# Conditioning in steps of 512 columns, and the first MLP's shift beside the first output projection

## The chip, the cores and the metric

The kernel runs on one core of a Trainium2 chip. Its time is the device time of one execution in microseconds (us). Matrix products run on TensorE (PE; its weight loads are shown apart as PEld), elementwise work on VectorE (DVE), ScalarE (ACT) and GpSimd (POOL). SyncE (SP) issues all DMA transfers here, in one queue and in order. Work moves between DRAM, the on-chip SBUF (128 partitions) and PSUM, which takes the results of matmuls in eight banks.

## What is computed

One inference step of a two-layer encoder on 1024 prompt tokens and 32 sample tokens, with 1024 features. Layer 0 has an mLSTM mixer, layer 1 banded attention, and each has a squared-ReLU MLP with 4096 hidden features. Every sublayer is modulated by six vectors (two shifts, two scales, two gates) that come from a conditioning vector c, of which there is one for the prompt and one for the sample:

```python
def ada_mod(c, w, b):
    return jax.nn.silu(c) @ w + b

for l in range(DEPTH):
    sh1, sc1, g1, sh2, sc2, g2 = jnp.split(ada_mod(c, p['w_ada'][l], p['b_ada'][l])[:, None, :], 6, axis=-1)
    u = x * (1 + sc1) + sh1
    y = mixer(u) if l == 0 else attention(u, k_sh, v_sh)   # ends with the output projection
    x = layer_norm(ALPHA * x + (1 + g1) * y, p['ln_g'][l, 0], p['ln_b'][l, 0])
    u = x * (1 + sc2) + sh2
    f = jnp.square(jax.nn.relu(u @ p['w_up'][l])) @ p['w_down'][l]
    x = layer_norm(ALPHA * x + (1 + g2) * f, p['ln_g'][l, 1], p['ln_b'][l, 1])
```

w_ada[l] has 1024 rows and 6144 columns, six parts of 1024. A further matrix of 2048 columns, w_ada_kv, conditions the keys and values that layer 1 reads. The parts are numbered 0 to 5 in the order sh1, sc1, g1, sh2, sc2, g2: the first MLP's shift is part 3 of layer 0.

## The kernel before

Activations are kept transposed, features on the partitions and tokens along the columns, in three token blocks of 384, 384 and 288 (TBS). Large products are made in three float32r passes (`proj`, L118 to L120): each operand is split into a high part, made by ACT (L89), and a remainder, made by DVE or POOL (L90).

**Conditioning.** Parts 0 and 1 of layer 0 are needed first, and TensorE makes them (`ada_start`). All other parts are made by `ada_cols` (L223) on DVE. It works on two chunks of 128 columns at a time: a block of 512 rows x 256 columns of the matrix is loaded (L229, 512 KB, into `raw`), and for each of its four row chunks and each of the two conditions the 256 columns are multiplied by one value of silu(c) per partition and added to an accumulator (L239 the first time, L236 after that). After the second block a transpose by 32 x 32 squares (L243) and a sum (L244) leave 16 columns in `cx`; when four such groups are in `cx`, four small matmuls with the matrix `sel` (L250) finish the sum over the partitions, and L253 adds the bias and writes eight chunks of `ada`. `ada_fix` makes 1 + scale and (1 + gate) / alpha; `combine` (L268) merges the layer norm's gain and bias with scale and shift into `comb`.

**Side work.** What is not the main sequence of products is written as generators under `Flow`. A generator yields the time, in us, that TensorE should spend on other work before its next step; the main sequence calls `flow.tick(us)` after each piece (1 us by default), and each tick moves a generator by at most one step. `flow.finish(g)` puts out all that is left of one. This sets the order in which the program is written down; the framework's scheduler then orders each engine's instructions and inserts the waits.

**The order around the change.** In the mixer (to about 440 us in the profile) query/key, value and output-gate projections alternate with `mlstm`, the chunks of the previous head. The rest of layer 0's conditioning, parts 2 to 5, runs beside it as `ada_l0` (L730): one buffer of the ring `wc`, named ada_room, is cut into accumulator, transposed copy and one block of loaded weights, and ADA_C gives the yields, 2.0 after each load and 2.0 at the end of a group. L790 finishes all that is left of it. Next, `combine` runs (L1044), and the first output projection `out_proj` (L958) begins: it loads its eight weight blocks (raw_oa) through the ring `raw`, which has three buffers, loads the residual `acc` (L808) and walks the three token blocks, with eight tiles of 24 matmuls for each. After a tile, L947 adds it to the residual, and `flow.tick(n / 96)` counts 4 us, or 3 in the last block. After a block its `norm` (L825) is started as side work: a sum over the features on DVE, the mean by a matmul (L843), squares, the variance by a matmul, and then in four steps the normalised residual and its modulation by `comb` (L324 to L329), which writes U, the input of the MLP; W00 holds its yields. `tmp_t` gives out five temporary buffers. The MLP's first products `up` read U in the order of the blocks.

The conditioning of layer 1 and of the keys and values (`ada_rest`, L1058) is side work of the first MLP, with loads through `raw`, temporaries from `tmp_t` and the yields ADA_B.

The lines of the program that the change touches:

Of the kernel before, what the change touches and what calls it, by code (L numbers as in the profile page):

```python
# [8 lines left out]
F32 = mybir.dt.float32  # L9
F32R = mybir.dt.float32r  # L10
AF = mybir.ActivationFunctionType
ALU = mybir.AluOpType
# [5 lines left out]
KC = D // P                     # feature chunks  # L18
TP = 1024                       # prompt tokens
TS = 32                         # sample tokens  # L20
T = TP + TS
NT = T // P + 1                 # token tiles, the last one holds the sample
# [4 lines left out]
NH = 4                          # mLSTM heads  # L27
CH = 128                        # mLSTM chunk
NCK = TP // CH
SAMPLE_C = NCK                  # index of the sample's mLSTM chunk  # L30
# [3 lines left out]
def segs(t0, n):  # L34
    """Pieces (offset, length, conditioning column) of a token block."""
# [11 lines left out]
class Flow:  # L47
    """Side work, as generators that yield how long (us) the tensor engine should do something else first."""
# [27 lines left out]
def trunk_kernel(ctx: ExitStack, tc: tile.TileContext, a, o):  # L76
# [6 lines left out]
    # ------------------------------------------------------------------ tools  # L83
# [3 lines left out]
    def split(dst_h, dst_l, src, eng=None):  # L87
        """dst_h + dst_l == src exactly, both parts in float32r."""
        nc.scalar.copy(dst_h, src)  # L89
        (eng or nc.vector).tensor_sub(dst_l, src, dst_h.bitcast(F32))  # L90

    def wtile(name, srcs, ncols=256, pool=None, eng=None, between=None):
        """A block of 4 contraction chunks x ncols columns, split. srcs: (dst slice fn, dram ap)."""
# [12 lines left out]
    def wblock(name, src, r0, c0, eng=None):  # L106
        """rows r0..r0+511, columns c0..c0+255 of src."""
# [3 lines left out]
    def proj(ps, n, halves, j, mov):  # L111
        """ps[:, :n] = the 128 columns j of the weight halves times mov(hl, k), three f32r passes."""
# [9 lines left out]
    # one activation table set serves every function used below  # L122
    nc.scalar.preload_act_table_set("natural_log_exp_and_others")

    # -------------------------------------------------------------- constants
    ident = cp.tile([P, P], F32, name="ident")
    make_identity(nc, ident)
    sel = cp.tile([P, 32], F32, name="sel")             # sel[32 a + j, j] = 1
# [8 lines left out]
    # x0T / x1T: the residual stream, transposed, while the mixers need its room  # L137
# [6 lines left out]
    # ------------------------------------------------- per-feature parameters  # L144
# [10 lines left out]
    comb = cp.tile([P, 3, KC, 2, 2], F32, name="comb")   # fused norm scale / shift per (norm, chunk, cond)  # L155
# [29 lines left out]
    def bank(name):  # L185
        """All eight banks in turn, for the phases that need no classes of them."""
# [19 lines left out]
    # silu(c) = c * exp(min(c, 0) - ln(1 + exp(-|c|)))  # L206
# [1209 lines left out]
```

## Time and profile before

| | us |
|---|---|
| median of 3 runs | 2562.2 |
| lowest, highest | 2561.2, 2562.53 |
| profiled execution, first to last instruction (its span) | 2562.6 |
| PE busy | 2493.5 |
| DVE busy | 1686.0 |
| ACT busy | 895.3 |
| POOL busy | 339.5 |

For the profiled execution the span is the only time of its own that is recorded; it lies 0.4 us above the median of the timed runs. Times are counted from the first instruction of the span. In a row of a group of instructions stand line, engine, operation, the tiles it writes and reads, shape and count, then the time busy and the mean duration in ns, and then the idle time of the engine just before them with what ended it. In a row of waits stand who waited, for whom, the sum in us, how often, and the longest. In a row of windows stand the stretch, then busy time and number of instructions of PE, PEld, DVE, ACT and POOL, the granted clock of TensorE as a share of full speed, the busy share of the DMA engines, and GB/s; asked for one tile, it has the engines alone that work on it. In a row of the timeline stand start, duration, engine, line, operation, and in brackets the idle time before it and what ended it.

### The profile page before, as it was taken

How to read it: one execution, taken by the hardware profiler on the slowest of the kernel's cores; microseconds unless marked ns; L12 is line 12 of the kernel's file. 1: busy time of each engine (PE TensorE's matmuls, PEld its weight loads, DVE VectorE, ACT ScalarE, POOL GpSimd, SP SyncE). 2: the span in 40 equal slices, each digit the busy share in tenths (PEclk: the TensorE clock that was granted, in tenths of full speed). 3: DMA queues.
4: the chain of work that ended last, by engine and by line, in shares of the span. 5: the costliest groups of instructions: out<-in, count | busy, mean ns of one | idle time of the engine just before them, and what ended most of it. 6: DMA issues, size and time to landing. Idle time of an engine off the chain costs nothing.

```text
span 2562.6 us, 40022 instructions
## 1 busy us (share of the span) xinstructions
PE 2493.5 (97%) x15784; PEld 2371.5 (93%) x15784; DVE 1686.0 (66%) x3825; ACT 895.3 (35%) x1903; POOL 339.5 (13%) x455
## 2 busy tenths in 40 slices
PE   7999999999999999999989999999999999999998
PEld 3899899999999999999989876789999999999997
DVE  3899999778679678766696676637644334343437
ACT  3654456242212211221256566625411211221212
POOL 0111100251000000000053143405300000000003
PEclk9999999999999999999999999999999999999999
DMA  7532323412224224223113400051111111111101
GB/s 235 161 91 88 93 82 110 142 34 84 89 91 131 92 86 137 83 91 120 58 68 116 97 4 1 1 159 34 50 50 42 42 50 42 49 51 41 44 31 68
DMA packets 192064, 201.20 MB, mean 79 GB/s; under 512 B 9337, under 2 KB 180749, under 8 KB 191877
## 3 DMA queue, kind: packets, MB, share of 16 engines
q1 hardware_dynamic: 191876, 198.65, 25.4%
q8 instruction: 124, 2.03, 0.3%
q14 instruction: 64, 0.52, 0.1%
HBM read 183.38 MB, written 17.60 MB: 78 GB/s over the span
## 4 chain that ended last, share of the span: by engine, by line
PE 82%; DVE 7%; DMA 2%; ACT 2%; issue 1%; POOL 1%; SPq 0%; ACTq 0%; DVEq 0%; POOLq 0%
PE dn L118 10%; PE up L118 9%; PE dn L120 9%; PE up L119 9%; PE up L120 9%; PE dn L119 9%; PE pv L1275 3%; PE s L1225 2%; PE pt L1255 2%; DVE ada_room L236 1%; DMA ada_room<-in_w_ada_dram 1%; PE o L118 1%; PE o L120 1%; PE o L119 1%; PE q L118 1%
## 5 line engine op out<-in xcount | busy, mean ns | idle before, releaser
L118 PE MATMUL dn<-h,w_dn 128*128 128x384 f32 (+2 forms) x1568 | 505.9, 323 | 0.0
L120 PE MATMUL dn<-h,w_dn 128*128 128x384 f32 (+2 forms) x1568 | 501.9, 320 | 0.0
L119 PE MATMUL dn<-h,w_dn 128*128 128x384 f32 (+2 forms) x1568 | 497.8, 318 | 0.0
L955 DVE SCALAR_TENSOR_TENSOR acc<-dn,ada,acc 128x384 f32<-128x384 f32 (+5 forms) x536 | 243.7, 475 | 235.8 <-PE dn L120 234.1
L118 PEld LDWEIGHTS dn<-h,w_dn 128*128 128x128 f32 x1568 | 294.5, 188 | 0.8 <-PE yt L914 0.2
L119 PEld LDWEIGHTS dn<-h,w_dn 128*128 128x128 f32 x1568 | 294.2, 188 | 0.1
L120 PEld LDWEIGHTS dn<-h,w_dn 128*128 128x128 f32 x1568 | 294.0, 188 | 0.0
L995 DVE TENSOR_TENSOR r<-r 128x384 f32<-128x384 f32 (+1 forms) x192 | 104.2, 544 | 282.7 <-ACT h L994 282.1
L993 ACT ACTIVATE r<-up 128x384 f32<-128x384 f32 (+1 forms) x192 | 88.9, 463 | 470.6 <-PE up L120 456.2
L118 PE MATMUL up<-U,w_up 128*128 128x384 f32 (+1 forms) x768 | 250.2, 326 | 0.0
L119 PE MATMUL up<-U,w_up 128*128 128x384 f32 (+1 forms) x768 | 249.1, 324 | 0.0
L120 PE MATMUL up<-U,w_up 128*128 128x384 f32 (+1 forms) x768 | 248.7, 324 | 0.0
L118 PE MATMUL up<-u,w_up 128*128 128x384 f32 (+1 forms) x768 | 248.5, 324 | 0.0
L119 PE MATMUL up<-u,w_up 128*128 128x384 f32 (+1 forms) x768 | 248.4, 323 | 0.0
L120 PE MATMUL up<-u,w_up 128*128 128x384 f32 (+1 forms) x768 | 248.3, 323 | 0.0
L89 ACT CAST w_up<-raw_up 128x1024 fp32r<-128x1024 f32 x64 | 66.9, 1049 | 411.1 <-PE dn L120 274.3
L236 DVE SCALAR_TENSOR_TENSOR aacc<-rada,cs,aacc 128x256 f32<-128x256 f32 x448 | 190.4, 478 | 0.0
L118 PEld LDWEIGHTS up<-U,w_up 128*128 128x128 f32 x768 | 145.1, 189 | 0.1
L120 PEld LDWEIGHTS up<-U,w_up 128*128 128x128 f32 x768 | 145.1, 189 | 0.0
L119 PEld LDWEIGHTS up<-U,w_up 128*128 128x128 f32 x768 | 145.1, 189 | 0.0
L120 PEld LDWEIGHTS up<-u,w_up 128*128 128x128 f32 x768 | 144.3, 188 | 0.0
L119 PEld LDWEIGHTS up<-u,w_up 128*128 128x128 f32 x768 | 144.2, 188 | 0.0
(317 smaller groups left out, 5403.0 us busy)
## 6 DMA issues: line engine op xcount, KB each, us to landing
raw_up<-in_w_up_dram SPq DMA_DIRECT2D x64, 512.0 KB
raw_dn<-in_w_down_dram SPq DMA_DIRECT2D x64, 512.0 KB
rada<-in_w_ada_dram SPq DMA_DIRECT2D x48, 512.0 KB
ada_room<-in_w_ada_dram SPq DMA_DIRECT2D x32, 512.0 KB
rada<-in_w_ada_dram SPq DMA_DIRECT2D x32, 256.0 KB
rada<-in_w_ada_kv_dram SPq DMA_DIRECT2D x16, 512.0 KB
acc<-xsp SPq DMA_DIRECT2D x4, 1536.0 KB
rc<-rc_d SPq DMA_DIRECT2D x8, 528.0 KB
```

Of the source, the lines that this page charges most:

```text
L89: nc.scalar.copy(dst_h, src)
L118: nc.tensor.matmul(ps, wh, mov(0, k), start=(k == 0), stop=False)
L119: nc.tensor.matmul(ps, wh, mov(1, k), start=False, stop=False)
L120: nc.tensor.matmul(ps, wl, mov(0, k), start=False, stop=(k == nk - 1))
L236: nc.vector.scalar_tensor_tensor(acc[:, cnd], raw[:, k], sc, acc[:, cnd], op0=ALU.mult, op1=ALU.add)
L955: nc.vector.scalar_tensor_tensor(xs, ps[:, off + o:off + o + mm_], gate[:, fc, cnd:cnd + 1], xs, op0=ALU.mult, op1=ALU.add)
L993: nc.scalar.activation(r, ps[:, :n], AF.Relu)
L995: nc.vector.tensor_mul(r, r, r)
L1225: nc.tensor.matmul(s[:, b, :w], qst, kk[i][:, g, k0 + j0:k0 + j0 + w], start=(i == 0), stop=(i == 1))
L1255: nc.tensor.transpose(pt[:kp, j - j0, pr * P:(pr + 1) * P], ps_[pr][:, j * P:j * P + kp], ident)
L1275: nc.tensor.matmul(pv[64 * e:64 * e + 64, :nq], V[:kp, vt0 + j, g * 64:(g + 1) * 64], pts[e][:kp, j, :nq], start=(j == 0), stop=(j == nt - 1))
```

## The change

`ada_cols` works on four chunks of 128 columns at a time. A load is 256 rows x 512 columns, still 512 KB, and there are four of them to a group in place of two. For each of the two row chunks of a load, and each condition, one operation on 512 columns takes the place of operations on 256. Each condition has an accumulator of its own, and its own transpose and sum at the end of a group, so that two groups now fill `cx` and lead to the `sel` matmuls. Of the yields two are left: step[0] after each load, step[1] at the end of a group; the one in the middle of a block is gone.

Beside the mixer `ada_l0` makes parts 2, 5 and 4 only, in this order. Its transposed copies now lie where the loaded weights lie in the room. Part 3, the first MLP's shift, is made by a new generator, `ada_shift`, which is side work of the first output projection, loads through the ring `raw` and takes its temporaries from `tmp_t`. It ends with the `combine` that stood ahead of the projection. The norms of that projection get a hook, `before`, that finishes `ada_shift` just ahead of their modulation. `ada_rest` uses the new `ada_cols` with yields of 5.0 and 2.0. Everything else in the diff is comments.

```diff
-    def ada_cols(src, c0, base, nch, mk, tmp_f, step, raw_f=raw_tile):
-        """ada[:, base..base+nch-1] = silu(c) @ src[:, c0..c0+128*nch-1] + bias, multiplied on the vector engine."""
-        for j in range(0, nch, 2):
-            acc = tmp_f([P, 2, 256], f"aacc_{base}_{j}")
-            for half in range(2):
-                raw = raw_f([P, 4, 256], f"rada_{base}_{j}_{half}")
-                nc.sync.dma_start(raw, src[512 * half:512 * half + 512, c0 + j * P:c0 + (j + 2) * P].rearrange(
+    def ada_cols(src, c0, base, nch, mk, tmp_f, step, raw_f):
+
+
+        cx3 = cx.rearrange("p g b -> p (g b)").rearrange("p (g b) -> p g b", g=2)
+        for j in range(0, nch, 4):
+            accs_ = [tmp_f([P, 512], f"aacc{cnd}_{base}_{j}", cnd) for cnd in range(2)]
+            for quarter in range(4):
+                raw = raw_f([P, 2, 512], f"rada_{base}_{j}_{quarter}")
+                nc.sync.dma_start(raw, src[256 * quarter:256 * quarter + 256, c0 + j * P:c0 + (j + 4) * P].rearrange(
                     "(k p) c -> p k c", p=P))
                 yield step[0]
-                for k in range(4):
+                for k in range(2):
                     for cnd in range(2):
-                        sc = cs[:, 4 * half + k, cnd:cnd + 1]
-                        if half or k:
-                            nc.vector.scalar_tensor_tensor(acc[:, cnd], raw[:, k], sc, acc[:, cnd],
+                        sc = cs[:, 2 * quarter + k, cnd:cnd + 1]
+                        if quarter or k:
+                            nc.vector.scalar_tensor_tensor(accs_[cnd], raw[:, k], sc, accs_[cnd],
                                                            op0=ALU.mult, op1=ALU.add)
                         else:
-                            nc.vector.tensor_scalar(acc[:, cnd], raw[:, k], sc, None, op0=ALU.mult)
-                    if k == 1 and step[1]:
-                        yield step[1]
-            at = tmp_f([P, 512], f"aat_{base}_{j}")
-            nc.vector.transpose(at, acc.rearrange("p c n -> p (c n)"))
-            nc.vector.tensor_reduce(out=cx[:, j // 2 % 4], in_=at.rearrange("p (b i) -> p b i", i=32), axis=mybir.AxisListType.X,
-                                    op=ALU.add)
-            yield step[2]
-            if j // 2 % 4 == 3:
+                            nc.vector.tensor_scalar(accs_[cnd], raw[:, k], sc, None, op0=ALU.mult)
+            for cnd in range(2):
+                at = tmp_f([P, 512], f"aat{cnd}_{base}_{j}", 2 + cnd)
+                nc.vector.transpose(at, accs_[cnd])
+                nc.vector.tensor_reduce(out=cx3[:, j // 4 % 2, 16 * cnd:16 * cnd + 16],
+                                        in_=at.rearrange("p (b i) -> p b i", i=32), axis=mybir.AxisListType.X, op=ALU.add)
+            yield step[1]
+            if j // 4 % 2:
                 ps = mk(f"adas_{base}_{j}")
                 for q in range(4):
                     nc.tensor.matmul(ps[32 * q:32 * q + 32, :16], sel, cx.rearrange("p g b -> p (g b)")[:, q::4],
                                      start=True, stop=True)
-                b0 = base + j - 6
+                b0 = base + j - 4
                 nc.vector.tensor_tensor(
-                    ada[:, b0:b0 + 8, :].rearrange("p (g b) c -> p g b c", g=4),
-                    ps[:, :16].rearrange("p (g c b) -> p g b c", g=4, c=2),
-                    pt2[:, b0:b0 + 8].rearrange("p (g b) -> p g b", g=4)[:, :, :, None].broadcast_to([P, 4, 2, 2]),
+                    ada[:, b0:b0 + 8, :].rearrange("p (g b) c -> p g b c", g=2),
+                    ps[:, :16].rearrange("p (g c b) -> p g b c", g=2, c=2),
+                    pt2[:, b0:b0 + 8].rearrange("p (g b) -> p g b", g=2)[:, :, :, None].broadcast_to([P, 2, 4, 2]),
                     op=ALU.add)
...
-    ADA_C = (2.0, 0.0, 2.0)
+    ADA_C = (2.0, 2.0)
...
     def ada_l0():
         room = ring.tile([P, 2112], F32, tag="wc", name="ada_room", bufs=6)
 
         def raw_f(shape, name):
-            return room[:, 1024:2048].rearrange("p (k c) -> p k c", k=4)
-
-        def tmp_f(shape, name):
-            return room[:, 512:1024] if len(shape) == 2 else room[:, :512].rearrange("p (k c) -> p k c", k=2)
-        yield from ada_cols(a["w_ada"][0], 2048, 16, 32, adat, tmp_f, ADA_C, raw_f)
+            return room[:, 1024:2048].rearrange("p (k c) -> p k c", k=2)
+        def tmp_f(shape, name, i):
+            return room[:, 512 * i:512 * i + 512]
+        for part in (2, 5, 4):
+            yield from ada_cols(a["w_ada"][0], part * D, part * KC, KC, adat, tmp_f, ADA_C, raw_f)
         ada_fix(0, [(2, "g"), (4, "sc"), (5, "g")])
     flow.add(ada_l0())
...
-    ADA_B = (4.0, 2.0, 1.0)
+    ADA_B = (5.0, 2.0)
     NOW = True
+    ADA_S = (3.0, 1.0, 4.0)
...
-        def norm(ti, ni, nm, w, after=None):
+        def norm(ti, ni, nm, w, after=None, before=None):
...
             nc.vector.tensor_mul(w2[:, 0], w1[:, 0], w1[:, 1])
+            if before:
+                before()
             for i in range(0, KC, 2):
...
-    combine(0, lng(0), lnb(0), ada_part(0, 4), ada_part(0, 3))
     norms = {}
 
+    def ada_tmp(shape, name, i):
+        return tmp_t(shape, name)
+
+    def ada_shift():
+        yield from ada_cols(a["w_ada"][0], 3 * D, 3 * KC, KC, mm, ada_tmp, ADA_S, raw_tile)
+        combine(0, lng(0), lnb(0), ada_part(0, 4), ada_part(0, 3))
+    shift = flow.add(ada_shift(), ADA_S[2])
+
     def end_out0(ti):
-        norms[ti] = flow.add(norm(ti, 0, f"n00_{ti}", W00), now=NOW)
+        norms[ti] = flow.add(norm(ti, 0, f"n00_{ti}", W00, before=lambda: flow.finish(shift)), now=NOW)
...
     def ada_rest():
-        yield from ada_cols(a["w_ada"][1], 0, 48, 48, mm, tmp_t, ADA_B)
-        yield from ada_cols(a["w_ada_kv"], 0, 96, 16, mm, tmp_t, ADA_B)
+        yield from ada_cols(a["w_ada"][1], 0, 48, 48, mm, ada_tmp, ADA_B, raw_tile)
+        yield from ada_cols(a["w_ada_kv"], 0, 96, 16, mm, ada_tmp, ADA_B, raw_tile)
```

## The prediction

> **What bounds the kernel now.** I began with the page's summary, then cut the span into stages by windows, because an average over 2562.6 us says nothing about the two places that the change touches.
>
> ```profile
> span 2562.6 us, 40022 instructions
> ...
> PE 2493.5 (97%) x15784; PEld 2371.5 (93%) x15784; DVE 1686.0 (66%) x3825; ACT 895.3 (35%) x1903; POOL 339.5 (13%) x455
> ```
>
> TensorE (PE) is the bound, 97% busy. VectorE (DVE) can only matter where PE waits for it. The windows below are the mixer (62 to 440 us), the start of the first output projection, its rest with the first norms (up to 604), and the part of the first MLP that computes the second layer's conditioning.
>
> ```profile
> core 0: us, PE busy (x) PEld busy (x) DVE busy (x) ACT busy (x) POOL busy (x), PEclk, DMA share, GB/s
> 62.00:120.00 58.00, 54.47 (x354) 50.60 (x353) 49.10 (x99) 37.37 (x75) 9.73 (x15) 0.97 0.62 183
> 120.00:440.00 320.00, 315.76 (x2082) 297.48 (x2081) 292.87 (x870) 170.34 (x464) 34.06 (x100) 0.99 0.31 92
> 440.00:476.00 36.00, 34.50 (x201) 33.51 (x200) 28.02 (x63) 8.19 (x10) 2.72 (x2) 1.00 0.73 235
> 476.00:512.00 36.00, 36.00 (x211) 35.87 (x211) 28.27 (x39) 13.36 (x21) 12.63 (x10) 1.00 0.11 33
> 512.00:556.00 44.00, 39.33 (x241) 38.30 (x240) 37.89 (x59) 20.84 (x32) 28.43 (x20) 0.90 0.16 49
> ...
> 604.00:1184.00 580.00, 580.00 (x3637) 578.38 (x3637) 448.29 (x991) 121.48 (x197) 0.00 (x0) 1.00 0.33 102
> ```
>
> PE's idle time is small everywhere: 3.5 and 4.2 us in the mixer, 1.5 us at the start of the projection, 4.7 us around 512 to 556, none in the MLP. In the mixer DVE is nearly as full as PE (292.9 of 320 us). A stall costs more than its idle time, because the granted clock falls with it:
>
> ```profile
> 100.00:120.00 20.00, 17.58 (x103) 17.20 (x102) 18.34 (x29) 8.87 (x19) 8.44 (x9) 0.91 0.30 91
> 260.00:280.00 20.00, 17.83 (x100) 16.91 (x99) 16.32 (x48) 6.65 (x19) 2.08 (x7) 0.91 0.18 58
> ```
>
> A mean clock of 0.91 over 20 us is 1.8 us lost, twice in the mixer; 0.90 over 44 us in the norms is 4.4 us. The waits that stand behind the idle time are these, first in the mixer and then in 440 to 604 us:
>
> ```profile
> PE cu L638 <- DVE hn L664: 3.9, 6, 2.2
> PE ae_ps L527 <- ACT stk L520: 2.4, 1, 2.4
> DVE ada_room L236 <- DMA ada_room<-in_w_ada_dram: 10.8, 6, 3.2
> DVE ada_room L239 <- DMA ada_room<-in_w_ada_dram: 1.5, 3, 1.0
> ```
>
> ```profile
> PE mean_n L843 <- ACT sr_n L89: 4.5, 2, 2.5
> PE op_a L118 <- ACT w_oa L89: 1.5, 1, 1.5
> ```
>
> The multiply-adds of conditioning (L236 and L239 on the tile ada_room) make DVE, which takes its instructions in order, stand still for their loads for 12.3 us; the mixer's own DVE work is queued behind them. The longest PE wait shows it:
>
> ```profile
> 267.12 0.48 DVE L236 SCALAR_TENSOR_TENSOR ada_room<-ada_room,cs 128x256 f32<-128x256 f32 x1 [1.86 <-DMA ada_room<-in_w_ada_dram]
> ```
>
> ```profile
> 270.09 0.53 DVE L664 TENSOR_SCALAR hn<-num,sm 128x256 f32<-128x256 f32 x1
> ```
>
> The head's result hn comes at 270.6 us, behind a multiply-add that waited 1.86 us for its load, and PE waits for hn; the clock dip of 260 to 280 us follows.
>
> **The change, part by part.** First the price of the multiply-adds.
>
> ```profile
> L236 DVE SCALAR_TENSOR_TENSOR ada_room<-ada_room,cs 128x256 f32<-128x256 f32 x224 | 100.0, 478 | 10.8 <-DMA ada_room<-in_w_ada_dram 10.8
> L559 DVE SCALAR_TENSOR_TENSOR y<-qkp,pt,y 128x1059 f32<-128x1059 f32 x24 | 31.7, 1320 | 0.0
> L243 DVE STREAM_TRANSPOSE ada_room<-ada_room 128x512 f32<-128x512 f32 x16 | 11.2, 699 | 0.0
> L244 DVE TENSOR_REDUCE cx<-ada_room 128x16 f32<-128x512 f32 x16 | 10.8, 674 | 0.0
> L239 DVE TENSOR_SCALAR ada_room<-ada_room,cs 128x256 f32<-128x256 f32 x32 | 10.7, 346 | 5.5 <-DMA ada_room<-in_w_ada_dram 5.5
> ```
>
> No operation of this kind has 512 columns, so I take it on the line between the rows of 256 and 1059 columns: (1320 - 478) / 803 = 1.05 ns a column, 478 + 256 x 1.05 = 746 ns. It is bounded by 478 and by 2 x 478 = 956. [...]
>
> A group of 512 columns is then 14 x 0.746 + 2 x 0.69 (L239 at most doubles) + 2 x 0.70 + 2 x 0.67 = 14.6 us, where two groups of 256 columns take 2 x (14 x 0.478 + 2 x 0.346 + 0.70 + 0.67) = 17.5 us. Layer 0's conditioning is 132.7 us now (the four rows of ada_room). Afterwards six groups, 87.6 us, are in the mixer and two, 29.2 us, beside the output projection. Now it lies here (DVE time of ada_room):
>
> ```profile
> 62.00:120.00 58.00, 8.27 (x18) 0.97 0.62 183
> 120.00:440.00 320.00, 107.29 (x233) 0.99 0.31 92
> 440.00:476.00 36.00, 16.39 (x38) 1.00 0.73 235
> ```
>
> So the mixer loses 8.3 + 107.3 - 87.6 = 28.0 us of DVE work, and the projection gains 29.2 - 16.4 = 12.8 us.
>
> *The mixer's steps.* After L740 the mixer has 73 ticks: 6 in the first query/key projection, 13, 15 and 15 for the heads 1 to 3, 12 in each half of the o projection. The side work now needs 16 groups x 3 yields x 2 ticks = 96, so its last quarter is put out by the finish at L790, which is the 16.4 us after 440 us. Afterwards it needs 6 x 5 x 2 = 60 ticks and ends inside. The loads keep their size (512 KB) with rows of 2 KB in place of 1 KB; 24 in place of 32 pass through the one room, so there are fewer places where DVE can stand behind one. Against that, the transposed copies now lie in the loaded block's place, so at each of six groups the next load, and on SP what is queued behind it, waits 2 x (0.70 + 0.67) = 2.74 us longer; of the five yields to a group it is the one at the end, 2 ticks, that hides this. What I count: the waits of PE for hn, 3.9 us, and the 1.8 us of clock behind them, 5.7 us. Not counted are the 2.4 us of ae_ps and the first clock dip, whose chain is the gate rows. The bound above is all visible idle time and both dips, 3.5 + 4.2 + 3.6 = 11.3, with what is hidden in the matmuls' own durations:
>
> ```profile
> L118 PE MATMUL qk<-U,w_qk 128*128 128x384 f32 x128 | 45.6, 356 | 0.0
> ...
> L118 PE MATMUL up<-U,w_up 128*128 128x384 f32 x384 | 130.4, 340 | 0.0
> ```
>
> The same shape is 16 ns slower in the mixer than in the MLP; over the 3 x 128 of them that is at most 6 us, so 17 us. The bound below is 0 less 3: a burst is now four multiply-adds of 746 ns at a time and up to 2.98 + 2.74 us at a group's end, and work behind it can be that late once. I take 5.7, because it is what named waits show.
>
> *The start of the projection.* SP issues in order, and there the side loads stand in front of others:
>
> ```profile
> 446.28 1.30 SPq L808 DMA_DIRECT2D acc<-xsp  x2
> 452.15 0.37 SPq L229 DMA_DIRECT2D ada_room<-in_w_ada_dram  x1
> 452.57 1.13 SPq L808 DMA_DIRECT2D acc<-xsp  x1
> ...
> 465.00 0.37 SPq L229 DMA_DIRECT2D ada_room<-in_w_ada_dram  x1
> 465.47 0.45 SPq L96 DMA_DIRECT2D raw_oa<-in_w_out_a_dram  x1
> ```
>
> The third residual load and the last weight blocks leave behind loads that waited for DVE's multiply-adds. Without them the transfers begin some 5 us earlier, and the 1.5 us that PE waits for w_oa go. The new eight loads of the shift come behind all eight raw_oa in program order, ahead of raw_up; each takes one of three raw slots, so raw_up is held until the shift's sixth block is used.
>
> ```profile
> 539.71 0.33 PE L118 MATMUL up<-U,w_up 128*128 128x384 f32 x1
> ```
>
> Its product w_up is first read at 539.7 us, 70 us on, and that delay is covered; were it not, it would show as a PE wait for w_up.
>
> *The shift beside the projection.* Started after 4 us of ticks, it moves one step at each projection tile (4 us against yields of 3 and 1) and ends at tile 11 of 24. The first norm modulates at tile 13, so the added finish finds nothing left to do. The 12.8 us of DVE work fall where DVE idles: 8.0 and 7.7 us in 440 to 512, and 6.1 in 512 to 556. I take 0 for it, between a gain of 4.5 (the mean's waits, if DVE, freed of the mixer's leftovers, arrives earlier) and a loss of 12.8 with 1.8 of clock (all of it in front of the norms).
>
> *The second layer's conditioning* falls from 32 x 8.7 to 16 x 14.6 us of DVE, some 45 us less. PE is busy for 580 of 580 us there, so nothing comes of it; the cover is PE itself. If a burst of 5.7 us delayed a bank's release, it would cost, but eight banks stand between, each a tile of 12 matmuls of 580 / 3637 = 0.16 us, 15 us together. The sel matmuls keep their number; combine, ten small operations, moves with the shift.
>
> Sum: 5.7 + 1.5 = 7.2 us from the profiled 2562.6 gives 2555.4; the median of the runs is 0.4 lower than that span, so 2555.
>
> **The rivals.** *Nothing measurable happens*: PE's waits in the mixer are for the heads' own chains and only the 1.5 us go, 2561. For it: the largest single wait, ae_ps, does not involve the change. Against: the 12.3 us that DVE stood at its loads. Chance 0.22.
>
> *The norms come late* (the other side). Two means of the norms already make PE wait, 4.5 us together (the row of mean_n above), and DVE is at 37.9 of 44 us there. The shift's loads queue behind 4 MB of residual and the last raw_oa, so its multiply-adds may start near 465 us and run into the first norm, which also shares five temporary tiles with the shift's four. If all 12.8 us reach those two matmuls, with 1.8 of clock: 2555 + 14.6 = 2570. It outweighs the gain from 7.2 us of delay on, and is measurable beyond 12.3. Against it stands the slack of norm 0:
>
> ```profile
> 513.23 0.61 DVE L329 TENSOR_TENSOR U<-ut_n,U 128x384 fp32r<-128x384 f32 x1 [0.57 <-POOL ut_n L326]
> ```
>
> Its last product is written at 513.8 us and first read at 539.7 (the row of PE above), so 12.8 us more would not reach PE through norm 0 itself, only through the norms queued behind it. Chance 0.23. [...]
>
> *PE runs free*: all 17 us of the mixer's bound, 1.5 and half of the 4.5 go, 2562 - 21 = 2541. For it: DVE at 92% in the mixer, relieved by 28 us. Against: hardly any PE wait there is longer than 1 us. Chance 0.12.
>
> **How the numbers follow.** The forecast has 0.43 and alone spans 2549 to 2559. From this kernel's spread of 1.3 us over its runs I take 0.2%, 5.1 us, as what can be told from no change: faster is below 2557. Of the forecast 0.40 lies below it and 0.03 above; with 0.12 that is 0.52 faster. Same has 0.22 + 0.03 and the 0.02 of late norms that just cancel, 0.27; slower 0.21. The range leaves out the far ends of the last two rivals: 2543 to 2569.
>
> **What would show it.** Right: L236 of ada_room x84 near 746 ns; DVE below 270 of 320 us in the mixer; no PE wait for hn over 1 us; no w_oa wait; the shift's last multiply-add before 500 us. Wrong: PE waits for sr_n or qr_n that sum to more than 8 us between 480 and 600, a wait for comb or w_up, a lower clock there, or a new PE idle time in the MLP.

## The result and the profile after

The changed kernel takes 2586.3 us (median of four runs, 2583.4 to 2587.8) where the kernel before takes 2562.4 beside it: a ratio of 1.0097, with an interval of 1.0084 to 1.0109. It is 24 us slower. The forecast was 2555, with a range up to 2569.

The page of the changed kernel, its span and its engines. It executes fewer instructions than before, and VectorE is busy for 44 us less.

```profile
span 2586.0 us, 39645 instructions
...
PE 2500.7 (97%) x15784; PEld 2377.7 (92%) x15784; DVE 1642.1 (64%) x3441; ACT 897.0 (35%) x1903; POOL 342.3 (13%) x455
```

The same windows as those shown of before (busy time of each engine, then the granted clock, the DMA share and GB/s):

```profile
120.00:440.00 320.00, 315.96 (x2082) 297.33 (x2081) 273.43 (x754) 171.75 (x462) 34.49 (x100) 0.99 0.29 85
440.00:476.00 36.00, 36.00 (x207) 36.00 (x206) 23.69 (x37) 4.87 (x6) 0.00 (x0) 1.00 0.72 237
476.00:512.00 36.00, 33.00 (x185) 32.06 (x184) 32.31 (x49) 9.34 (x14) 6.09 (x3) 0.95 0.30 89
512.00:556.00 44.00, 34.95 (x225) 34.13 (x224) 36.05 (x51) 21.47 (x34) 29.40 (x20) 0.88 0.16 49
556.00:604.00 48.00, 43.90 (x252) 43.52 (x251) 33.00 (x64) 25.49 (x58) 22.80 (x25) 0.96 0.00 1
604.00:1184.00 580.00, 577.64 (x3623) 573.68 (x3622) 422.71 (x745) 126.27 (x205) 0.00 (x0) 1.00 0.36 110
```

VectorE lost 19.4 us of work in the mixer (292.9 to 273.4), and TensorE's idle time there went from 4.24 to 4.04 us: nothing. The first stretch of the projection has no idle time left. The norms are where it was lost: TensorE idles 3.0 us in 476 to 512, 9.1 in 512 to 556 and 4.1 in 556 to 604, at a lower clock. And the MLP, full before, lacks 2.4 us. The waits behind the norms, in 440 to 604 us (total, times, longest); before, the two of mean_n were 4.5 us:

```profile
PE mean_n L847 <- ACT sr_n L89: 12.3, 3, 7.0
PE mean_n L847 <- DVE sr_n L90: 2.4, 2, 1.8
PE var_n L847 <- ACT qr_n L89: 1.4, 1, 1.4
```

Where each stage begins tells the same without busy times. The first matmul of each stage, in the two profiled executions (us):

| first matmul of | before | after | lost since the row above |
|---|---|---|---|
| the first output projection | 438.51 | 437.86 | -0.65 |
| the first MLP, up | 539.71 | 550.49 | +11.4 |
| the first MLP, down | 604.22 | 615.51 | +0.5 |
| layer 1's queries | 1293.95 | 1310.32 | +5.1 |
| layer 1's keys and values | 1401.23 | 1418.69 | +1.1 |
| the attention's scores | 1464.39 | 1486.36 | +4.5 |
| the end of the span | 2562.6 | 2586.0 | +1.4 |

The rows sum to 23.4 us, the difference of the spans. They compare one execution with one other, so a row of 1 us or less says little. There are three places: the norms, one spot in the MLP, and one in the keys and values.

### The profile page after: what moved, and what is told of

Its sections match the earlier page's. It is cut to its first block, busy times and chain, and to the rows that moved or that the text cites. A ratio compares the mean times of both kernels' runs of the same rounds, so it can differ in the third digit from the quotient of the medians.

```text
span 2586.0 us, 39645 instructions
## 1 busy us (share of the span) xinstructions
PE 2500.7 (97%) x15784; PEld 2377.7 (92%) x15784; DVE 1642.1 (64%) x3441; ACT 897.0 (35%) x1903; POOL 342.3 (13%) x455
## 5 line engine op out<-in xcount | busy, mean ns | idle before, releaser
L238 DVE SCALAR_TENSOR_TENSOR aacc<-rada,cs,aacc 128x512 f32<-128x512 f32 x252 | 178.4, 745 | 0.3 <-DMA rada<-in_w_ada_kv_dram 0.3
```

Of the source, the lines that this page charges most:

```text
L238: nc.vector.scalar_tensor_tensor(accs_[cnd], raw[:, k], sc, accs_[cnd], op0=ALU.mult, op1=ALU.add)
```

## The experiments: which part costs

Each part was made alone, with the other two as in the kernel before. All times below are medians beside runs of the kernel before on the same chip, and the difference is to those.

**The shift alone is moved**, at 256 columns everywhere:

```diff
-        yield from ada_cols(a["w_ada"][0], 2048, 16, 32, ...)
+        for part in (2, 5, 4):
+            yield from ada_cols(a["w_ada"][0], part * D, part * KC, KC, ...)
+    shift = flow.add(ada_shift(), ADA_S[2])    # 256 columns, beside the projection
```

> All conditioning keeps its steps of 256 columns; only the shift is moved beside the first output projection. Theory N (the shift's work on VectorE ahead of the norms makes TensorE wait for their means): about 11 us of the 24 come back, 2573, with the first up product near 550 us in place of 539.7. Theory W (the wide steps are what costs, through the order and the buffers of the first MLP and what follows): 2562, up near 540.

2573.1 us, 12.8 above the kernel before. At 256 columns the shift has four groups, and in the trace its last multiply-adds end at 507.7 us, later than in the changed kernel (492.1).

**The mixer's conditioning alone takes 512 columns**, with the shift left in it:

```diff
-        yield from ada_cols(...256 columns...)
+        for part in (2, 3, 4, 5):
+            yield from ada_cols(...512 columns...)
```

> Only layer 0's conditioning beside the mixer takes 512 columns; the shift stays there and layer 1's conditioning keeps 256. Theory N: 2560 to 2562, since the changed kernel's projection started only 0.65 us earlier; up near 539. Theory W: above 2562 if wide steps cost wherever they stand, by a third of the 12 us that were lost behind the norms, 2566.

2561.2, 0.9 above, with an interval of the ratio of 0.9996 to 1.0015: no gain that can be measured. This mixer makes part 3 as well; the mixer without it comes up again under the prediction.

**Layer 1's conditioning alone takes 512 columns**:

```diff
-        yield from ada_cols(a["w_ada"][1], 0, 48, 48, ...256 columns, 4.0, 2.0, 1.0...)
+        yield from ada_cols(a["w_ada"][1], 0, 48, 48, ...512 columns, 5.0, 2.0...)
```

> Only layer 1's conditioning, beside the first MLP, takes 512 columns. Theory N: 2562, nothing is lost before or after the norms. Theory W: the 12 us that the changed kernel loses behind the first up products come here, 2574, with 5 us of it between the first down product and the first query product.

2568.2, 7.9 above. **The changed kernel with layer 1 back at 256 columns**, the reverse of that edit:

> The changed kernel with layer 1's conditioning back at 256 columns: layer 0 wide and the shift moved. Theory N alone: 2586 less at most 2, since all of the loss would follow from the moved shift. Theory W: 2574, the loss behind the norms is gone and the 11 us in them stay.

2575.8, 15.5 above. The three parts alone, 12.8 + 0.9 + 7.9 = 21.6, nearly make the 24. Two causes are to be found: the shift's place, and layer 1. The kernel at 15.5 is the base of the experiments on the shift.

## The experiments: why the shift costs

Two halves of the shift's work were left out in turn. **No loads**: the multiply-adds read columns of U, already on the chip, so the shift is wrong.

```diff
-                nc.sync.dma_start(raw, src[256 * quarter:256 * quarter + 256, ...])
+                # raw is a view of U
```

> The same kernel with the shift's multiply-adds kept and its eight loads left out: they read columns of U in place of the weights, so the shift is wrong. Theory D: 2573 to 2576, nothing comes back. Theory Q: 2564 to 2567, w_up is split near 475 us again and no sum of the norms takes over 1.5 us for 384 columns.

**No multiply-adds**: the loads stay, each block is touched by one small operation, and the shift is zero.

> Layer 0 wide, the shift moved, layer 1 at 256 columns, as in the run that took 2575.8; here the shift's eight loads stay but its multiply-adds, transposes and sums are left out (eight columns of each load are read, the shift is zero). Theory D (the 29 us of VectorE work ahead of the norms cost the time): 2562, the whole 15 us come back. Theory Q (the loads push the MLP's first weights back, so that GpSimd splits them while the norms run): 2573 to 2576, the means still wait.

2563.2 and 2562.9 us, 2.2 and 1.9 above. Either half gone takes nearly the whole cost with it, so it is neither the transfers nor the VectorE time as such. What is left is when the multiply-adds run: without loads they start at 444.2 us. (That edit also brings the first two w_up remainders forward, to 464 us from 481 in the base; two runs below take this up.) VectorE in the changed kernel, in order of time (s_n is a norm's sum over the features and sr_n its split for the matmul of the mean; q_n and qr_n are the same for the squares and the variance):

```profile
461.20 0.88 DVE L241 TENSOR_SCALAR aacc<-rada,cs 128x512 f32<-128x512 f32 x2 [0.31 <-DMA rada<-in_w_ada_dram]
...
479.99 0.95 DVE L850 TENSOR_TENSOR s_n<-acc 128x768 f32<-128x768 f32 x1
...
482.25 0.75 DVE L238 SCALAR_TENSOR_TENSOR aacc<-rada,cs,aacc 128x512 f32<-128x512 f32 x1
...
485.57 2.72 DVE L90 TENSOR_TENSOR sr_n<-s_n,sr_n 128x384 fp32r<-128x384 f32 x1
...
489.41 2.72 DVE L238 SCALAR_TENSOR_TENSOR aacc<-rada,cs,aacc 128x512 f32<-128x512 f32 x4
...
502.88 0.55 DVE L90 TENSOR_TENSOR qr_n<-q_n,qr_n 128x384 fp32r<-128x384 f32 x1
...
526.02 0.47 DVE L953 SCALAR_TENSOR_TENSOR acc<-op_a,ada,acc 128x256 f32<-128x256 f32 x1
526.41 2.30 DVE L853 TENSOR_TENSOR s_n<-s_n 128x384 f32<-128x384 f32 x1
...
529.35 2.00 DVE L90 TENSOR_TENSOR sr_n<-s_n,sr_n 128x384 fp32r<-128x384 f32 x1
```

The answering operations of the kernel before:

```profile
480.88 0.96 DVE L846 TENSOR_TENSOR s_n<-acc 128x768 f32<-128x768 f32 x1
...
485.53 0.56 DVE L90 TENSOR_TENSOR sr_n<-s_n,sr_n 128x384 fp32r<-128x384 f32 x1 [0.58 <-ACT sr_n L89]
...
495.15 0.56 DVE L90 TENSOR_TENSOR qr_n<-q_n,qr_n 128x384 fp32r<-128x384 f32 x1 [0.64 <-ACT qr_n L89]
...
517.76 0.56 DVE L90 TENSOR_TENSOR sr_n<-s_n,sr_n 128x384 fp32r<-128x384 f32 x1 [0.24 <-ACT sr_n L89]
```

The first multiply-add waits for its load until 461.2 us. The first norm's sum begins on time (479.99 against 480.88), but the second half of the multiply-adds lies between its steps, and their transposes and sums run to 494 us. That norm's variance is ready for its matmul at 503.4 in place of 495.7, and the second norm's sum at 531.4 in place of 518.3: 13 us late, of which TensorE waits 7.0. VectorE has no idle time from 461.5 to 503.9 us, so the temporary buffers that the norm shares with the shift held nothing up. The second delay is larger than the first because the last operations have become longer, 2.30 and 2.00 us for what takes 0.56. GpSimd's queue in the changed kernel shows why: it makes the remainders of the w_up blocks just then.

```profile
485.16 2.71 POOL L90 TENSOR_TENSOR w_up<-raw_up,w_up 128x1024 fp32r<-128x1024 f32 x1 [98.81 <-ACT w_up L89]
...
525.26 5.67 POOL L90 TENSOR_TENSOR w_up<-raw_up,w_up 128x1024 fp32r<-128x1024 f32 x2
```

In the list of VectorE above, the operations on sr_n, of 2.72 and 2.00 us, end 0.4 us after such a GpSimd operation does (487.87 and 530.93), and that of 2.30 ends near the middle of the row of two, while L953, which adds a product from PSUM to the residual, takes 0.47 in the midst of it. Beside the remainders, 0.55 us have become 2.0 to 2.7; in the run below that makes them on VectorE, the last step of the second norm's sum takes 0.54 us and the sr_n of both norms 0.56, while the same addition from PSUM still takes 0.47. The kernel before has such collisions too, but its second sum is done before the remainders begin, and they hold the squares behind it, for which TensorE doesn't wait:

```profile
518.76 4.76 POOL L90 TENSOR_TENSOR w_up<-raw_up,w_up 128x1024 fp32r<-128x1024 f32 x2 [3.20 <-ACT w_up L89]
```

```profile
527.17 2.18 DVE L863 TENSOR_TENSOR q_n<-q_n 128x384 f32<-128x384 f32 x1
```

GpSimd's own queue is not what makes the second norm late. Before GpSimd's next operation of that norm it stands idle, and waits for VectorE:

```profile
550.29 1.23 POOL L327 TENSOR_SCALAR ut_n<-acc,comb 128x384 f32<-128x384 f32 x1 [9.32 <-DVE acc L881]
```

**The six remainders on VectorE in place of GpSimd**, in the base and, as a control, in the kernel before:

```diff
-                                          nc.gpsimd if g == 0 or (g == 1 and pr == 0) else None) ...
+                                          nc.gpsimd if l and (g == 0 or (g == 1 and pr == 0)) else None) ...
```

> The same kernel complete, but the remainders of the first MLP's first weight blocks (w_up of layer 0) are made on VectorE in place of GpSimd, six times 1.2 us of VectorE work in place of six times 2.4 us of GpSimd's. Theory D: 7 us more work on the engine that is behind, 2576 to 2583. Theory Q: the 0.55 us operations that took 2.0 to 2.85 us beside GpSimd's splits take 0.55 again, 8.8 us less against 7.3 more, not all of it in the norms' way: 2569 to 2574.

> The kernel before with the same single edit. Here only two operations of the norms are stretched, by 3.1 us together (2.18 and 2.10 us in place of 0.56). Theory Q: 2558 to 2562. Theory D: 7 us more VectorE work near the norms, 2564 to 2568.

2568.0 (7.0 above) and 2564.6 (3.7 above). With the remainders on GpSimd, the base costs 15.5 us more than the kernel before; with them on VectorE, 2568.0 stands 3.3 above 2564.6. (The control's 3.7 us fall where the second of its two theories, more VectorE work near the norms, had put them.) The profiled executions agree: from the projection's first matmul to the MLP's first, base and kernel before take 112.4 and 101.2 us, and with the remainders on VectorE 103.4 and 103.3. So most of the price of the shift's place is paid through these collisions. **Only the last four of the six**:

> The same kernel of 2575.8 us, with the pace as it is, and only the last four of the first MLP's six early w_up remainders on VectorE in place of GpSimd (all six gave 2568.0). If it is the last four, at 521 to 537 us, that hold VectorE's short operations in the second norm's sum, the gain is the same: 2566 to 2570. If the first two, at 481 to 491 us, carry it, it stays at 2574 to 2578.

2569.4, 7.9 above: it is the last four, in the second norm, that carry it. The first two do not, as the next run also shows, in which **the first two w_up blocks are loaded and split ahead of the shift's loads**:

```diff
+        if (pr, half) == (3, 1):
+            up_pre[0, 0] = [wblock(f"up0_0_0_{i}", a["w_up"][0], 512 * i, 0, nc.gpsimd) for i in range(2)]
```

> Mixer and shift as in the changed kernel with the second layer at 256 columns (2575.8 us, 15.5 above the kernel before), but the first two of the MLP's w_up blocks are loaded and split ahead of the shift's loads. It takes apart two ways in which the shift's late loads reach the norms. If it is the first two GpSimd splits (481 and 489 us, inside the first norm's sums), they now come before 470 us, norm 0's mean is one stretch again, and the time falls to 2566 to 2570. If it is the shift's multiply-adds themselves, which run to 490 us and now start some 3 us later, or the last four splits, the time stays at 2574 to 2579.

2577.8, 18.3 above. The two remainders came at 462 us, clear of the norm, and nothing was gained, but the multiply-adds came later still: they start at 464.0 us, against 457.2 in the base, and their last transpose ends at 495.8. So the run shows that moving the first two is not enough, not what they cost by themselves. Its waits in 440 to 604 us:

```profile
PE mean_n L884 <- ACT sr_n L89: 16.0, 3, 6.8
```

What makes the multiply-adds late? First guess, **their pace**: a tick each 4 us moves one step, and ten steps reach into the norm. Twice the pace:

```diff
+        for i, us in enumerate(ada_cols(... ADA_S, raw_tile)):
+            if i % 2 == 0:
+                yield us
```

> Mixer and shift as in the changed kernel, second layer at 256 columns (2575.8 us, 15.5 above the kernel before), with the shift's side work at twice the pace: only every second yield is kept, so that all its multiply-adds are written down, and stand in VectorE's order, ahead of the first norm's sum. The loads and the work are the same. If the cost is that the second half of the multiply-adds is interleaved with the first norm's sums (476 to 494 us), which moves each later step of the norms by 8 to 13 us, this recovers most of it: 2561 to 2566. If the loads alone are too late to be used before the norm (the eighth comes in at about 473 us), or the multiply-adds cost wherever they stand beside the projection, it stays above 2571.

2576.5, 15.0 above: the guess is wrong. The trace says why, first VectorE, then TensorE's waits:

```profile
459.33 0.88 DVE L241 TENSOR_SCALAR aacc<-rada,cs 128x512 f32<-128x512 f32 x2 [0.24 <-DMA rada<-in_w_ada_dram]
...
482.36 1.31 DVE L244 STREAM_TRANSPOSE aat<-aacc 128x512 f32<-128x512 f32 x2
...
487.02 0.94 DVE L887 TENSOR_TENSOR s_n<-acc 128x768 f32<-128x768 f32 x1
```

```profile
PE mean_n L884 <- ACT sr_n L89: 9.5, 2, 6.6
PE adas L251 <- DVE cx L245: 6.6, 1, 6.6
```

The start didn't move, because the load wasn't there. From 459.3 the two groups run almost without a gap to 484.8, and the first norm's sum begins at 487.0, where the kernel before has it at 480.9; TensorE now waits for the sums cx as well. The two groups take 25.5 us here and cannot be done between 459 and 481. SP's queue in the changed kernel shows what stands ahead of the loads, the residual and the last block of raw_oa, for which SP waits until 450 us:

```profile
442.36 3.78 SPq L811 DMA_DIRECT2D acc<-xsp  x3
446.18 4.07 SPq L96 DMA_DIRECT2D raw_oa<-in_w_out_a_dram  x1
450.35 26.95 SPq L231 DMA_DIRECT2D rada<-in_w_ada_dram  x8
```

Second guess, **the place of the loads** in SP's queue: the residual's second and third blocks, 2.75 MB, are loaded behind the shift's first blocks in place of ahead of them, at the old pace and at twice the pace.

```diff
-        for ti in order:
-            nc.sync.dma_start(accs[ti], xsp[l][:, :, t0:t0 + n])
+        load(0)
+        # load(1) 12 us of ticks later (8 at twice the pace), load(2) another 12 us later
```

> Mixer and shift as in the changed kernel, second layer at 256 columns, the shift at its own pace (2575.8 us), but the second and third blocks of the residual (2.75 MB, first used some 35 and 70 us later) are loaded behind the first blocks of the shift in place of ahead of them. The theory now: the shift's 29.2 us of multiply-adds cannot begin before their first load lands, at 457 to 459 us, behind the residual and the last raw_oa, and so cannot be done before the first norm's sum is due at 476 to 481. With the residual's 2.75 MB out of the way the first load lands some 10 us earlier, near 447 to 449. At this pace the second half of the multiply-adds is still written between the first norm's sums, so part of the cost stays: 2565 to 2572. If it stays at 2576, the time at which the loads land is not what counts.

> The same with the shift at twice the pace (2576.5 us without the residual's move), so that all multiply-adds stand ahead of the first norm's sum in VectorE's order. If they start near 448 us they end near 478 and the first norm is late by at most 3 us: 2562 to 2568, no TensorE wait of 6.6 us for the sums cx. If VectorE still waits for loads until 455 or later, 2572 or more.

2566.4 at the old pace, 4.6 above, with a ratio of 1.0022 (1.0011 to 1.0033); 2569.8 at twice the pace, 8.1 above. The start of the multiply-adds in the base, and then, in VectorE's order, the run at the old pace:

```profile
457.18 0.89 DVE L241 TENSOR_SCALAR aacc<-rada,cs 128x512 f32<-128x512 f32 x2 [0.33 <-DMA rada<-in_w_ada_dram]
```

```profile
451.40 0.88 DVE L241 TENSOR_SCALAR aacc<-rada,cs 128x512 f32<-128x512 f32 x2
...
484.94 1.29 DVE L244 STREAM_TRANSPOSE aat<-aacc 128x512 f32<-128x512 f32 x2
```

The multiply-adds start at 451.4, and 10.9 of the 15.5 us are gone by the medians, with nothing of the shift's own work changed. By the profiled executions it is less: from the projection's first matmul to the MLP's first takes 101.2 us before, 112.4 in the base and 107.7 here. TensorE still waits 9.3 us for mean_n there, against 12.3, and the same operations are still stretched (2.71 us for the first norm's sr_n, 2.53 for the second norm's sum); that this is all of the rest was not shown. The faster pace, which was expected to be better, is not: the two intervals overlap (1.0020 to 1.0039 at twice the pace).

So the chain is shown link by link: loads behind the residual, multiply-adds that begin at 457 to 461 us, a first norm whose variance is some 8 us late, and a second norm whose sums fall on the w_up remainders. The links overlap (by the medians, mending the first is worth 10.9 us, the last 7.6), and their shares were not separated further.

## The experiments: why layer 1 costs

In the run with layer 1 alone at 512 columns, TensorE has one long wait in the whole MLP from 620 us on, at 1072 us. ScalarE there:

```profile
1072.27 0.41 ACT L1034 ACTIVATE r<-up 128x288 f32<-128x288 f32 x1 [2.14 <-PE up L120]
1072.71 0.44 ACT L1035 ACTIVATE h<-r 128x288 fp32r<-128x288 f32 x1
1073.06 2.92 ACT L89 CAST w_dn<-raw_dn 128x1024 fp32r<-128x1024 f32 x3
```

The wait, and a window around it:

```profile
PE dn L118 <- ACT w_dn L89: 1.9, 1, 1.9
```

```profile
1070.00:1080.00 10.00, 7.91 (x40) 7.17 (x39) 6.13 (x8) 4.27 (x7) 0.00 (x0) 0.83 0.33 100
```

Three blocks of w_dn are converted at once, behind the last up tile, when the first down product already wants them. In the kernel before the first of them is converted 9 us ahead of the down product:

```profile
1062.08 1.05 ACT L89 CAST w_dn<-raw_dn 128x1024 fp32r<-128x1024 f32 x1 [1.63 <-DMA raw_dn<-in_w_down_dram]
```

What stands ahead of raw_dn in SP's queue now is the table of relative-position bias. The generator of layer 1's conditioning builds it when it has finished, and with fewer steps it finishes 133 us earlier. SP's queue of the same run:

```profile
1048.62 0.60 SPq L346 DMA_DIRECT2D bias_d<-e_d  x1
1049.27 26.47 SPq L96 DMA_DIRECT2D raw_dn<-in_w_down_dram  x4
```

2.3 MB are ahead of raw_dn, and in ScalarE's written order all four w_dn conversions of this group stand behind the last up tile. The blocks had landed before that: the DMA moves 1 GB/s in 1065 to 1070 us and nothing in 1070 to 1075. So TensorE waits for ScalarE's order of instructions and not for the data; that this order comes from the transfer in the way is a guess so far. Three runs test it. **The table back near its old place**, with layer 1 at 512 columns; **the table alone early** in the kernel before, all multiply-adds at 256 columns; and **the table back** in the whole change.

```diff
     def ada_rest():
         ...
-        yield
-        bias_table()
+    # called after down (0, group 6, column 4, block 0); for the early one after up (0, group 5, column 3, block 2)
```

> Only the second layer's conditioning at 512 columns, as in the 2568.2 us run (7.9 above the kernel before), but the table of relative-position bias, which the conditioning's generator builds when it is done, is written down where the kernel before has it (about 1174 us) and not where the faster conditioning brings it (1041 us). Theory B: the cost is that the table's 2.3 MB transfer now stands ahead of the MLP's w_dn blocks, so that ScalarE's conversions of w_dn are put behind the last up tile and PE waits 2.07 us at 1072 us, with a clock dip after it. By B that stall goes and the time is 2561, 0 to 2 us above the kernel before. Theory C, the longer multiply-add bursts cost wherever they are: it stays at 2568.

> The kernel before, all multiply-adds at 256 columns, with one change: the table of relative-position bias is built 133 us earlier, after the same up tile as in the run where the second layer's conditioning alone is at 512 columns (2568.2 us). Theory B (the table's place is what costs): slower than the kernel before by 2 to 6 us, with a PE wait for w_dn near 1071 us; in the written order one w_dn conversion still stands ahead of the last two up tiles here, so less than the full 5.4. Theory C (the bursts): no change, 2561.

> The changed kernel with the bias table back at about 1174 us. Theory B: the step of 4.0 us at 1070 us goes; whether the step of 4.4 us at 1430 us (PE waits for keys in the second layer's key/value products), which only the full change shows, goes with it is open. 2582 if only the first goes, 2578 if both do, 2586 by theory C.

2564.3 (4.8 above), 2570.6 (11.1 above) and 2578.6 (19.1 above). In the traces the table's transfer leaves SP at 1133 us in the first run and at 1145 in the third, where the kernel before has it at 1184. With it there, TensorE's wait of 1.9 us for w_dn is 0.3 us at most in the first run and is gone in the third. The early table costs by itself, more than forecast: in the kernel before it makes TensorE wait for w_up, whose block landed behind the table at 1066 us; the granted clock is 0.78 over 1060 to 1070 us. Its waits in 1040 to 1120 us:

```profile
PE up L118 <- ACT w_up L89: 4.9, 1, 4.9
PE dn L120 <- DVE w_dn L90: 1.0, 1, 1.0
```

From the MLP's first down product to layer 1's first query product the profiled executions take:

| | table late | table early |
|---|---|---|
| layer 1 at 256 columns | 689.7 (before) | 698.8 |
| layer 1 at 512 columns | 690.9 | 695.1 |
| whole change | 691.0 | 694.8 |

In this stretch the bursts of 512 columns cost about 1 us and the early table 4 to 9. The medians leave more to the bursts: with the table back, layer 1 at 512 columns is still 4.8 us above the kernel before beside it (ratio 1.0006 to 1.0024), though its profiled span, 2562.3, equals that of before. What makes up the rest of that median stays open. So does the step of 4.5 us in the keys and values of the changed kernel, with a wait of 2.7 us for uk, the input of that product: with the table back the step is 1.6 us, though the table isn't built there. The mixer alone at 512 columns has a step of 1.8 us there, and the shift or layer 1 alone at most 0.2; no run told why.

**All mendings together**: the whole change with the table back and the shift at twice the pace, and then also with the residual behind the shift's loads.

> The whole change (512 columns everywhere, the shift beside the projection) with both mendings: the shift at twice the pace, and the bias table back at about 1174 us. If the two causes found are all that costs, 2586.3 less 4.9 for the table and less 10 to 15 for the pace: 2562 to 2571. If it falls below 2559 the change pays after all once it is placed well; if it stays above 2575 a third cause is open.

> The whole change at 512 columns with the three mendings: the residual's later blocks behind the shift's loads, the shift at twice the pace, the bias table at its old place. By the theory as above: the time of the run with the first two mendings, and 0 to 5 us more for the second layer, 2563 to 2571; below 2557 it would beat the kernel before.

2578.1 (16.6 above) and 2573.4 (11.7 above). Both lie above what was expected, and the first above the 2575 from which a third cause was to be open: the step in the keys and values is one. Both contain the faster pace, which turned out to do no good; the table back and the residual moved, at the old pace, were not run together. No version came out below the kernel before.

## Why the prediction was wrong

**The price of a multiply-add was right.** 746 ns were forecast for 512 columns; the groups of the changed kernel beside the MLPs and in the mixer:

```profile
L238 DVE SCALAR_TENSOR_TENSOR aacc<-rada,cs,aacc 128x512 f32<-128x512 f32 x252 | 178.4, 745 | 0.3 <-DMA rada<-in_w_ada_kv_dram 0.3
...
L238 DVE SCALAR_TENSOR_TENSOR ada_room<-ada_room,cs 128x512 f32<-128x512 f32 x84 | 62.8, 761 | 7.0 <-DMA ada_room<-in_w_ada_dram 7.0
```

The forecast's groups are a little too long all the same, because durations in the trace overlap: 84 operations of 761 ns are busy for 62.8 us, and a whole group for 14.0 us in the mixer and 13.5 beside the MLP, where 14.6 was forecast.

**The mixer's gain of 5.7 us was mis-sized: it is 0.65 between these two executions, which is less than they scatter.** The step took the waits for hn, 3.9 us, and the clock dip behind them as the change's own. TensorE's waits for hn did fall to 1.4 us, but another of the same matmul came, for sm, of 1.88 us until 186.9; VectorE, in its order, had two weight remainders ahead of sm, and stood 2.06 us for ScalarE at the first. The dip of 260 to 280 us went (19.41 of 20 us, 1.00), and one stands at 180 to 200:

```profile
180.00:200.00 20.00, 18.12 (x113) 16.59 (x112) 14.15 (x40) 8.53 (x24) 4.02 (x9) 0.91 0.45 129
```

The other profiled executions say the same: with the old mixer (parts 2 to 5 at 256 columns, five runs) the projection begins at 436.0 to 438.5 us, 437.2 in the mean, and with the new one (parts 2, 5 and 4 at 512, thirteen runs) at 433.8 to 439.6, 437.0 in the mean. The rival "nothing measurable happens" described the mixer rightly.

**The 1.5 us at the start of the projection** went as forecast: 36.00 of 36 us busy.

**The step that failed is "The shift beside the projection", where the sum has 0.** It counted VectorE's idle time, 8.0 and 7.7 us in 440 to 512 us and 6.1 behind it, as room for 12.8 us more. But the first 20 us of it cannot be used, since the loads land only at 457 to 461 us behind the residual; in 440 to 476 VectorE is less busy than before, 23.7 of 36 against 28.0. Under its rival the forecast has the loads behind the residual and a start near 465 us, but it did not carry this into the sum. Nor do the ticks place the work ahead of the norm: they end at tile 11, about 44 us on, which is 482 us, and the first norm's sum was to start at 480.9. The measured price is 12.8 us alone and 15.5 with the wider mixer.

**The rival "the norms come late"** had the place, the late loads and the means that TensorE waits for, and its argument against, that the slack of norm 0 would pass a delay on only through the norms behind it, named the way it went. It did not have GpSimd's remainders, through which most of the price is paid. That its 12.8 us equal the 12.8 measured for the shift alone is luck: it counted added VectorE work. Its signs came true: waits for sr_n and qr_n of 16.1 us, a lower clock there, and idle time in the MLP.

**"That delay is covered", said of raw_up, looked at too little.** w_up was indeed ready when first read. But its making blocks others: the first two remainders, late by their loads, hold the first norm's sr_n for 2.72 us, which no run shows to cost anything. The last four, which do cost, are late by the norm ahead of them: GpSimd starts them without idle time behind the first norm's operations, at 525.26 us, and with the loads kept and the multiply-adds left out they begin at 516.25, as early as in the kernel before. The cover asked who reads the block, not whom its making blocks.

**"Nothing comes of it", said of layer 1's conditioning, was wrong by 7.9 us.** VectorE has 39 us less work there (254.6 to 215.8), in place of the 45 forecast, and as argued nothing comes of that. But the generator ends with the bias table, and what ends earlier starts its last step earlier, ahead of loads that had stood ahead of it. This is the loss that no case of the forecast held, and with the late norms it is why the time lies beyond the range. From 2555 to 2586.3 it is 31.3 us: 5.7 for the mixer, 12.8 for the shift alone and 7.9 for layer 1 alone make 26.4, and the other 5 are about as much as the step in the keys and values, whose cause is open.

## What to carry to other kernels

Idle time of an engine is room only from the moment at which the data of the moved work can be there; write down when its first load lands behind everything that the queue holds, and add the work to that time. When side work gets shorter, look at what its generator does at its end, and at what that passes on its way forward. A block made on GpSimd was not free beside VectorE here, where operations of 0.55 us took 2.0 to 2.7 while one was made: ask not only who reads the block, but what VectorE has to do in that time.

## What was not expected of the hardware

GpSimd's remainders in the norms, of 2.71 us for one and 5.67 for two, held VectorE's operations of 0.55 us for 2.0 to 2.7 us, and moving four of them to VectorE was worth 7.6 us. And the clock fell after single waits of 1.88 us (0.91 over 180 to 200 us) and 1.9 us (0.83 over 1070 to 1080 us), while one of 1.49 us at 466 to 468 us in the kernel before left it at 1.00. In steps of 2 us it stands at 0.65 and 0.50 from 188 to 192 us, and then at 0.99 and 1.00; with layer 1 alone at 512 columns it is 0.95 over 1070 to 1075 us, 0.71 over 1075 to 1080, and 1.00 over 1080 to 1090.
